# Weight block sums of seven-product tiles: from four GpSimd instructions to four transfers that add into SBUF

## The chip, the cores and the metric

The kernel runs on one core of one Trainium2 chip. The metric is the device time of one execution in microseconds; three runs of the kernel before give 1016.14, 1017.87 and 1018.72 us, median 1017.87. The engines are named as in the profile: PE (TensorE, the matrix products; PEld its weight loads), DVE (VectorE), ACT (ScalarE), POOL (GpSimd) and SP (SyncE). SP, ACT and POOL issue transfers (DMAs).

## The reference

One inference step of a one-layer decoder trunk, for 512 prompt tokens and 8 sample tokens together (520 columns), with width 1024. The mixer (gated recurrence and attention) is untouched by the change. What matters is the feed-forward part, with 2816 hidden features:

```
h2 = rms_norm(x, norm2_g) * (1.0 + sc2) + sh2
gu, up = jnp.split(h2 @ w_ffn_in, 2, axis=-1)
x = x + g2 * ((jax.nn.silu(gu) * up) @ w_ffn_out)
```

All inputs are float32.

## The kernel before

Activations lie with features on the 128 partitions and the 520 tokens along the row. Each float32 factor is split into a rounded part and a rest (`hi`, `lo`), and each product of two factors is three matmuls: hi·hi, lo·hi, hi·lo. A weight block is split by a cast on ACT (L270) and a subtraction on DVE (L271), in `split_four`, into a tile `wb` that holds four 128x128 blocks of `hi` and four of `lo`. The token factors are split the same way in `split`.

The feed-forward input product is done in 22 tiles of 128 hidden features (`jt` 0 to 21): each needs 128 gate columns and 128 up columns of `w_fi`, both 1024 rows deep. Tiles 0 to 3 are done plainly. Tiles 4 to 21, the fast tiles, use a scheme with seven products of half the depth in place of eight. A tile's weights form four blocks: A11 and A12 are the gate columns, rows 0-511 and 512-1023; A21 and A22 the up columns, rows 0-511 and 512-1023. The tokens likewise: `b1` and `b2` are features 0-511 and 512-1023 of `h2`, each with a left and a right half of 260 tokens (`L_`, `R_`). The scheme needs four sums of weight blocks (S1 to S4) and four sums of token blocks. The token sums are made once, for all tiles, by POOL in `h2_blocks` (four calls of four instructions, L1638 to L1644), then split by `split_blocks`. The weight sums are made in each tile by four POOL instructions (L261 to L264) into two buffers `ws`, when the tile's first block is split. Seven products (`BLOCKS`: A11, S2, S3, S1, A12, A22, S4), 12 matmuls each, accumulate into four PSUM banks X, Y, W, Z (`fi4x`, `fi4y` ... in the profile, the number being that of the tile). `fast_tile` combines the banks between the products, on DVE and ACT: after S1, Z is copied to `cp`, u2 is added to Z, and Y is written from `cp` and W; A22 then accumulates into W.

Between the seven products stand joined products: parts of the output product with `w_fo`, of 24 matmuls (`fo` in the profile, placed by the table `JOIN`): two in each of the tiles 4 to 16 and in 21, one in each of 17 to 20.

The order is set in the following way. The code asks for loads by `load_chunks` some 22 us, and for splits by `split_upto` some 11 us, ahead of use, by a reckoning of the matmuls in between (`reach`); a scheduler then puts each engine's instructions into one fixed order, and an engine goes through its own queue in that order, waiting where an operand or a buffer isn't there. Raw weights (`wraw`, 512 KB gate plus 512 KB up) alternate between two buffers, so a tile's load waits until the block A22 of the tile two before is split. The buffers `ws`, the raw joined weights of `w_fo`, the pairs `h2r` that `h2_blocks` reads, and earlier tiles share one ring of seven buffers (tag `pg`). All these loads go through SP's queue.

Of the kernel before, what the change touches and what calls it, by code (L numbers as in the profile page):

```python
# [8 lines left out]
F32 = mybir.dt.float32  # L9
# [3 lines left out]
ALU = mybir.AluOpType  # L13
# [11 lines left out]
KT = 8  # L25
# [40 lines left out]
def kernel(ctx, tc, xT, par, gates, b_f, cst, cse, own, cache_k, cache_v, cache_lf, pt,  # L66
# [3 lines left out]
    pe, act, dve, pool, sp = nc.tensor, nc.scalar, nc.vector, nc.gpsimd, nc.sync  # L70
# [3 lines left out]
    wp = ctx.enter_context(tc.tile_pool(name="wp", bufs=3))  # L74
    pgp = ctx.enter_context(tc.tile_pool(name="pgp", bufs=7))
# [79 lines left out]

    for c in range(len(chunks)):
        whole(c)
    joined = set()
    for jt in range(FF // 128):
        c = len(chunks)  # L160
        chunks.append(cols(w_fi, 128 * jt, 128) + cols(w_fi, FF + 128 * jt, 128))
        if jt < GROUP:
            whole(c)
            continue
        for name in BLOCKS:
            units.append((c, name, 4))
            if name in JOIN[jt]:
                g, i = JOIN[jt][name]
                if i % 2 == 0:
                    joined.add(len(chunks))  # L170
                    chunks.append(cols(w_fo, 128 * i, 256, 128 * GROUP * g, GROUP))
                units.append((max(joined), 128 * (i % 2), GROUP))
# [28 lines left out]
    def load_chunks(upto):  # L201
        while state["dma"] < len(chunks) and state["dma"] <= upto:
            c = state["dma"]
            if c in joined:
                raw = pgp.tile([128, GROUP, 256], F32, name="wraw", tag="pg")
            else:
                raw = wp.tile([128, KT, 256], F32, name="wraw", tag="wraw", bufs=2)
            o = 0
            for src, r0, nk, c0, n in chunks[c]:
                sp.dma_start(raw[:, :nk, o:o + n],  # L210
                             src[r0:r0 + nk * 128, c0:c0 + n].rearrange("(k p) c -> p k c", p=128))
                o += n
            raws[c] = raw
            state["dma"] += 1


    after = {}
# [4 lines left out]
    def split_upto(n):  # L222
        while state["split"] < len(units) and state["split"] <= n:
            m = state["split"]
            c, o, nk = units[m]
            load_chunks(c)
            raw = raws[c]
            state["split"] += 1
            if isinstance(o, str):
                splits[m] = split_block(raw, o)  # L230
                continue
            if c in joined:
                splits[m] = split_four(raw[:, :, o:o + 128])
                continue
            his, los = [], []
            step = 4 if m in in_heap else KT
            for k0 in range(0, nk, step):
                k1 = min(nk, k0 + step)
                if m in in_heap:
                    hi = slot("whs", 512, F32R).rearrange("p (k c) -> p k c", c=128)  # L240
                    lo = slot("wls", 512, F32R).rearrange("p (k c) -> p k c", c=128)
                else:
                    hi = wp.tile([128, KT, 128], F32R, name="whi", tag="whi", bufs=3)
                    lo = wp.tile([128, KT, 128], F32R, name="wlo", tag="wlo", bufs=3)
                src = raw[:, k0:k1, o:o + 128]
                state["act"] = act.copy(hi[:, :k1 - k0], src)  # L246
                with held(m):
                    state["last"] = dve.tensor_tensor(lo[:, :k1 - k0], src, hi[:, :k1 - k0].bitcast(F32), ALU.subtract)  # L248
                his += [hi[:, k] for k in range(k1 - k0)]
                los += [lo[:, k] for k in range(k1 - k0)]  # L250
            splits[m] = (his, los)

    blocks = {}

    def split_block(raw, name):
        if name == "A11":
            a11, a12, a21, a22 = (raw[:, k:k + 4, o:o + 128] for o in (0, 128) for k in (0, 4))
            s12, s34 = (pgp.tile([128, 8, 128], F32, name="ws", tag="pg") for _ in range(2))
            s1, s2, s3, s4 = s12[:, :4], s12[:, 4:], s34[:, :4], s34[:, 4:]
            blocks.update(A11=a11, A12=a12, A22=a22, S1=s1, S2=s2, S3=s3, S4=s4)  # L260
            pool.tensor_tensor(s1, a21, a22, ALU.add)  # L261
            pool.tensor_tensor(s2, s1, a11, ALU.subtract)
            pool.tensor_tensor(s3, a11, a21, ALU.subtract)
            pool.tensor_tensor(s4, a12, s2, ALU.subtract)  # L264
        return split_four(blocks[name])

    def split_four(src):
        state["tag"] = "wlo" if state.get("tag") == "whi" else "whi"
# [301 lines left out]
    raw = wraw()  # L570
# [1063 lines left out]
    def h2_blocks(k):  # L1634
        b1, b2 = h2raw[k], h2raw[k + 4]
        u, w = slot("u"), slot("w")
        with tc.issue_after(state["blocks"].ins) if k != 3 else nullcontext():
            first = pool.tensor_tensor(w[:, R_], b2[:, R_], b1[:, R_], ALU.subtract)  # L1638
        if k == 3:
            state["blocks"] = first  # L1640
        with tc.issue_after(state["blocks"].ins):
            pool.tensor_tensor(u[:, L_], b1[:, R_], b1[:, L_], ALU.subtract)
            pool.tensor_tensor(w[:, L_], b2[:, R_], u[:, L_], ALU.subtract)
            pool.tensor_tensor(u[:, R_], b2[:, L_], w[:, L_], ALU.subtract)  # L1644
        traw[k] = u, w

    def split_blocks(k0):
# [10 lines left out]
    def fast_tile(jt, ac):  # L1658
# [9 lines left out]
        for m_, name in enumerate(BLOCKS):  # L1668
            n = begin()
            hi, lo = splits[n]  # L1670
            for k in range(4):
                ah, al = h2_block(name, k)
                for m, (wt, at) in enumerate(((hi, ah), (lo, ah), (hi, al))):
                    state["mm"] = pe.matmul(into[name], lhsT=wt[k], rhs=at, start=m_ < 4 and k == 0 and m == 0,
                                            stop=k == 3 and m == 2, skip_group_check=m_ > 3)
            if name == "A11":
                act.copy(cp[:, L_], X)
            elif name == "S2":
                add(u2, cp[:, L_], Y)
            elif name == "S3":  # L1680
                add(W, u2, W)
            elif name == "S1":
                act.copy(cp[:, R_], Z)  # L1683
                add(Z, u2, Z)
                add(Y, cp[:, R_], W)
            elif name == "A12":
                act.activation(sw[:, L_], X, AF.Silu)
            elif name == "A22":
                close(W, L_)
            elif name == "S4":  # L1690
                act.activation(sw[:, R_], Z, AF.Silu)
                close(Y, R_)
            run_later(n)
            if name in JOIN[jt]:
                g, i = JOIN[jt][name]
                product(f"fo{g}_{i}", ac[GROUP * g:GROUP * g + GROUP], lambda j, b_, i=i: residual(i, b_, 5, j))
# [97 lines left out]
```

## Time and profile before

| what | us | 
|---|---|
| runs shown (three) | 1016.14, 1017.87, 1018.72 |
| the profiled execution: its span, first to last instruction | 1016.4 |
| PE busy | 994.3 (98%) |
| DVE busy | 797.3 (78%) |
| ACT busy | 547.5 (54%) |
| POOL busy | 327.6 (32%) |
| first fast tile's first product, on PE | from about 697 |
| last joined and output products, to the end | from about 970 |

The profiled execution's own device time isn't listed apart from the three; its span is what the page gives. The page has busy times by engine, busy shares in 40 slices of the span, the chain of work that ended last, the costliest groups of instructions, and the DMA issues. Other views of the same trace list instructions in order of time, waits, and busy times in a window. In a row of the timeline stand the start, the duration, the engine, the line of the kernel and out<-in by the program's names, and in brackets how long the engine was idle before and what ended that. The trace moved 206.97 MB at a mean of 204 GB/s, with the DMA engines less used in the feed-forward part than before it.

### The profile page before, as it was taken

Reading aid. Unit: us, or ns where it says so; the run is one execution under the profiler, and the core shown is the slowest. Engines: PE = TensorE matmul, PEld = TensorE weight load, DVE = VectorE, ACT = ScalarE, POOL = GpSimd, SP = SyncE. Lnnn points to the kernel's source line nnn. Section 1 sums busy time; section 2 is a strip of 40 time slices with the busy share of each in tenths; the row PEclk is TensorE's granted clock in tenths of the full one; section 3 lists DMA queues with packets and bytes.
Section 4 is the critical chain, followed back from the end, with each engine's and each line's share of the span. In section 5 each row is a group of like instructions: output and inputs, shape, how many; then the busy total and the mean of one; then the engine's idle time right before and its main releaser. Section 6 shows DMA issues by size and latency. Waiting matters only on the chain.

```text
span 1016.4 us, 21281 instructions
## 1 busy us (share of the span) xinstructions
PE 994.3 (98%) x8012; PEld 921.1 (91%) x8012; DVE 797.3 (78%) x1423; ACT 547.5 (54%) x1128; POOL 327.6 (32%) x415
## 2 busy tenths in 40 slices
PE   5999999999999999999999999999999999999996
PEld 2799999999998988888888888999999999999996
DVE  5559999998999888886655544869988888888764
ACT  4534576848761576777783233554444444445553
POOL 0346111121143245653400001583442442425112
PEclk9999999999999999999999999999999999999998
DMA  9798857788879998995867995324234243233122
GB/s 325 250 324 279 242 189 202 243 261 278 281 250 345 331 312 286 321 294 190 251 216 269 319 340 186 84 74 115 81 108 125 63 125 98 70 104 105 63 64 85
DMA packets 164378, 206.97 MB, mean 204 GB/s; under 512 B 9827, under 2 KB 125043, under 8 KB 164211
## 3 DMA queue, kind: packets, MB, share of 16 engines
q1 hardware_dynamic: 147634, 152.78, 48.1%
q0 software_dynamic: 12960, 46.41, 13.8%
q10 hardware_dynamic: 3680, 6.42, 1.7%
q8 instruction: 63, 1.03, 0.4%
q14 instruction: 41, 0.33, 0.1%
HBM read 192.49 MB, written 13.09 MB: 202 GB/s over the span
## 4 chain that ended last, share of the span: by engine, by line
PE 93%; DMA 2%; DVE 2%; ACT 1%; issue 0%; SPq 0%; POOL 0%; DVEq 0%; POOLq 0%; ACTq 0%
PE fo L307 12%; PE k L307 5%; PE wo L307 5%; PE gb L307 5%; PE gr L307 5%; PE v L307 5%; PE ga L307 5%; PE xr L307 5%; PE pb L307 4%; PE pv L839 3%; PE pa L307 3%; PE po L1302 2%; PE qp L542 2%; PE q L542 2%; PE ada L374 2%; PE ptt L1268 2%
## 5 line engine op out<-in xcount | busy, mean ns | idle before, releaser
L246 ACT CAST whi<-wraw 128x1024 fp32r<-128x1024 f32 (+1 forms) x79 | 82.0, 1039 | 113.6 <-PE pb L307 34.3
L248 DVE TENSOR_TENSOR wlo<-wraw,whi 128x1024 fp32r<-128x1024 f32 (+1 forms) x79 | 99.1, 1256 | 19.0 <-ACT whi L246 16.6
L307 PE MATMUL fo<-ach,wb 128*128 128x260 f32 x512 | 93.4, 283 | 0.0
L270 ACT CAST wb<-ws 128x512 fp32r<-128x512 f32 x72 | 44.7, 621 | 86.0 <-PE fo L307 58.9
L700 POOL DMA_DIRECT2D pg<-in_cache_k_dram x74 | 39.6, 536 | 143.1 <-DVE S L751 62.6
L271 DVE TENSOR_TENSOR wb<-wraw,wb 128x512 fp32r<-128x512 f32 x86 | 76.4, 889 | 4.7 <-ACT wb L270 3.9
L307 PEld LDWEIGHTS fo<-ach,wb 128*128 128x128 f32 x512 | 78.9, 188 | 0.0
L271 DVE TENSOR_TENSOR wb<-ws,wb 128x512 fp32r<-128x512 f32 x72 | 68.7, 954 | 12.6 <-ACT wb L270 11.0
L261 POOL TENSOR_TENSOR ws<-wraw 128x512 f32<-128x512 f32 x18 | 24.4, 1353 | 153.2 <-DMA wraw<-in_w_fi_dram 104.1
L307 PE MATMUL fo<-acl,wb 128*128 128x260 f32 x256 | 72.2, 282 | 0.0
L270 ACT CAST wb<-wraw 128x512 fp32r<-128x512 f32 x86 | 53.5, 622 | 31.4 <-ACT cp L1683 6.2
L750 DVE TENSOR_TENSOR pg<-pg,qb 128x1024 f32<-128x1024 f32 x48 | 57.9, 1221 | 2.5 <-DMA pg<-in_cache_k_dram 2.5
L751 DVE TENSOR_REDUCE S<-pg 128x16 f32<-128x1024 f32 x48 | 57.4, 1209 | 0.2
L1259 POOL TENSOR_SCALAR p<-p,mu 128x128 f32<-128x128 f32 (+3 forms) x28 | 38.4, 1381 | 53.0 <-DVE mu L1255 47.1
L307 PEld LDWEIGHTS fo<-acl,wb 128*128 128x128 f32 x256 | 48.2, 188 | 0.0
L1253 ACT ACTIVATE p<-p,mu 128x128 f32<-128x128 f32 (+3 forms) x64 | 35.4, 554 | 18.2 <-DVE mu L1252 18.0
L307 PE MATMUL v<-hh,whi 128*128 128x260 f32 x128 | 38.2, 298 | 0.8 <-ACT row L819 0.5
L307 PE MATMUL k<-hh,whi 128*128 128x260 f32 x128 | 37.3, 292 | 0.0
L307 PE MATMUL pb<-oh,whi 128*128 128x260 f32 x128 | 37.1, 290 | 0.2 <-ACT oh L1360 0.2
L307 PE MATMUL gb<-hh,whi 128*128 128x260 f32 x128 | 37.0, 289 | 0.0
L307 PE MATMUL v<-hl,whi 128*128 128x260 f32 x128 | 36.9, 288 | 0.0
L307 PE MATMUL v<-hh,wlo 128*128 128x260 f32 x128 | 36.9, 288 | 0.0
(1101 smaller groups left out, 3957.3 us busy)
## 6 DMA issues: line engine op xcount, KB each, us to landing
araw<-in_ada_w_dram SPq DMA_DIRECT2D x48, 512.0 KB, 7.6
wraw<-in_w_fi_dram SPq DMA_DIRECT2D x44, 512.0 KB, 5.3
pg<-in_cache_k_dram POOLq DMA_DIRECT2D x42, 512.0 KB, 6.2
pg<-in_cache_v_dram SPq DMA_DIRECT2D x42, 512.0 KB, 5.5
wraw<-in_w_in_dram SPq DMA_DIRECT2D x34, 512.0 KB, 6.4
wraw<-in_w_in_dram SPq DMA_DIRECT2D x11, 1024.0 KB, 8.5
pg<-in_cache_v_dram POOLq DMA_DIRECT2D x22, 512.0 KB, 6.1
pg<-in_cache_k_dram POOLq DMA_DIRECT2D x32, 256.0 KB, 5.9
```

Source lines behind the costliest of these rows:

```text
L246: state["act"] = act.copy(hi[:, :k1 - k0], src)
L248: state["last"] = dve.tensor_tensor(lo[:, :k1 - k0], src, hi[:, :k1 - k0].bitcast(F32), ALU.subtract)
L270: state["act"] = act.copy(t[:, :4], src)
L271: state["last"] = dve.tensor_tensor(t[:, 4:], src, t[:, :4].bitcast(F32), ALU.subtract)
L307: state["mm"] = pe.matmul(out[:, :t1 - t0], lhsT=wt[k], rhs=at, start=k == 0 and m == 0, stop=k == nk - 1 and m == 2)
L542: state["mm"] = pe.matmul(b[:, :HALF], lhsT=wt, rhs=at[:, t0:t1], start=k == 0 and m == 0, stop=k == 3 and m == 2)
L700: done.append(eng.dma_start(pg, cache[bass.ds(r, 1), :, c0:c1].rearrange("a p c -> (a p) c")))
L750: dve.tensor_tensor(pg, pg, q, ALU.mult)
L751: last = dve.tensor_reduce(S[r // 2][:, c:c + H], pg.rearrange("p (h d) -> p h d", d=DH), AX.X, ALU.add)
L839: pe.matmul(pv[0][32 * gq:32 * gq + 32, :], lhsT=pw[r][:, c:c + 32], rhs=pgs[gq // 2][:, 512 * hf:512 * hf + 512], start=j == 0, stop=j == ...
L1253: act.activation(p[:, :n + 128], p[:, :n + 128], AF.Exp, bias=mu[:, 0:1], scale=-1.0, accum_out=mu[:, 1:2])
L1259: (pool.tensor_scalar(p, p, mu[:, 2:3], None, ALU.mult) if a and i + 1 < KT else act.activation(p, p, AF.Copy, scale=mu[:, 2:3]))
```

## The change

The sums of weight blocks are no longer computed on POOL. A fast tile now makes four loads in place of two: the up block into the raw buffer, its rows 512-1023 (A22) a second time into a buffer `s1`, the gate block into the raw buffer, and the gate block a second time into a buffer that holds `s2` (rows 0-511, A11) and `s4` (rows 512-1023, A12). Then POOL issues four transfers of 256 KB inside SBUF that add to what lies at their target: A21 into `s1`, `s1` into `s2`, A11 into A21 (in the raw buffer itself, which becomes S3), and `s2` into `s4`. For the sums to be additions only, the scheme's signs are turned: S2 is S1 + A11 and no longer S1 - A11, S3 is A21 + A11 in place of A11 - A21, S4 is A12 + S2 in place of A12 - S2. The token sums and two of the combinations in `fast_tile` change sign to match. The buffers `s1` and `s2`/`s4` are taken when the load is asked for, no longer when the first block is split.

```
+            state["dma"] += 1
+            if c in fast:
+                raws[c] = load_fast(c)
+                continue
...
+    def load_fast(c):
+        raw = wp.tile([128, 2, KT, 128], F32, name="wraw", tag="wraw", bufs=2)
+        rows = [src[:, c0:c0 + n].rearrange("(k p) c -> p k c", p=128) for src, _, _, c0, n in chunks[c]]
+        s1, s24 = (pgp.tile([128, m, 4, 128], F32, name="ws", tag="pg") for m in (1, 2))
+        s1, s2, s4 = s1[:, 0], s24[:, 0], s24[:, 1]
+        a11, a12, a21, a22 = (raw[:, o, k:k + 4] for o in range(2) for k in (0, 4))
+        sp.dma_start(raw[:, 1], rows[1])
+        sp.dma_start(s1, rows[1][:, 4:])
+        sp.dma_start(raw[:, 0], rows[0])
+        sp.dma_start(s24.rearrange("p m k c -> p (m k) c"), rows[0])
+        pool.dma_start(s1, a21, accum_op=ALU.add)
+        pool.dma_start(s2, s1, accum_op=ALU.add)
+        pool.dma_start(a21, a11, accum_op=ALU.add)
+        pool.dma_start(s4, s2, accum_op=ALU.add)
+        return dict(A11=a11, A12=a12, A22=a22, S1=s1, S2=s2, S3=a21, S4=s4)
...
-                splits[m] = split_block(raw, o)
+                splits[m] = split_four(raw[o])
...
-            s12, s34 = (pgp.tile([128, 8, 128], F32, name="ws", tag="pg") for _ in range(2))
...
-            pool.tensor_tensor(s1, a21, a22, ALU.add)
-            pool.tensor_tensor(s2, s1, a11, ALU.subtract)
-            pool.tensor_tensor(s3, a11, a21, ALU.subtract)
-            pool.tensor_tensor(s4, a12, s2, ALU.subtract)
...
-            first = pool.tensor_tensor(w[:, R_], b2[:, R_], b1[:, R_], ALU.subtract)
+            first = pool.tensor_tensor(w[:, R_], b1[:, R_], b2[:, R_], ALU.subtract)
...
-            pool.tensor_tensor(u[:, L_], b1[:, R_], b1[:, L_], ALU.subtract)
-            pool.tensor_tensor(w[:, L_], b2[:, R_], u[:, L_], ALU.subtract)
-            pool.tensor_tensor(u[:, R_], b2[:, L_], w[:, L_], ALU.subtract)
+            pool.tensor_tensor(u[:, L_], b1[:, L_], b1[:, R_], ALU.subtract)
+            pool.tensor_tensor(w[:, L_], w[:, R_], b1[:, L_], ALU.subtract)
+            pool.tensor_tensor(u[:, R_], b2[:, L_], w[:, L_], ALU.add)
...
-                add(W, u2, W)
+                dve.tensor_tensor(W, W, u2, ALU.subtract)
...
-                add(Y, cp[:, R_], W)
+                dve.tensor_tensor(Y, W, cp[:, R_], ALU.subtract)
```

The change moves instructions in two queues. The orders of PE, DVE and ACT stay as they were, but that S3 is split out of `wraw`.

POOL's queue before, at the start of the fast tiles. `h2r` are the pairs of token blocks, `u` and `w` their sums (L1638 to L1644), `wraw_9988` the raw block of tile 4:

```order
L1506 TENSOR_TENSOR h2r_9412<-h2r_9412,mod_102 128x2x8
L1638 TENSOR_TENSOR w_9962<-h2r_9412,h2r_9386 128x260
L1642 TENSOR_TENSOR u_9961<-h2r_9386 128x260
...
L1643 TENSOR_TENSOR w_9980<-h2r_9412,u_9979 128x260
L261 TENSOR_TENSOR ws_10143<-wraw_9988 128x512
L1644 TENSOR_TENSOR u_9979<-h2r_9412,w_9980 128x260
L262 TENSOR_TENSOR ws_10143<-ws_10143,wraw_9988 128x512
L263 TENSOR_TENSOR ws_10144<-wraw_9988 128x512
L264 TENSOR_TENSOR ws_10144<-wraw_9988,ws_10143 128x512
```

The same place now (`ws_9989` is S1 of tile 4, `ws_9990` its S2 and S4; a row `DMA` is the issue of a transfer that adds; the lines are those of the changed kernel):

```order
L1512 TENSOR_TENSOR h2r_9412<-h2r_9412,mod_102 128x2x8
L230 DMA ws_9989<-wraw_9988 128x512
L1644 TENSOR_TENSOR w_9962<-h2r_9386,h2r_9412 128x260
L1648 TENSOR_TENSOR u_9961<-h2r_9386 128x260
...
L1649 TENSOR_TENSOR w_9980<-w_9980,h2r_9386 128x260
L231 DMA ws_9990<-ws_9989 128x512
L1650 TENSOR_TENSOR u_9979<-h2r_9412,w_9980 128x260
L232 DMA wraw_9988<-wraw_9988 128x512
L233 DMA ws_9990<-ws_9990 128x512
L230 DMA ws_10149<-wraw_10148 128x512
```

The first sum of tile 4 has moved from behind 15 of the 16 token block instructions to ahead of all of them; the second stands where the first stood.

SP's queue before, from tile 4 to tile 7 (`wraw_9988`, `10140`, `10392`, `10599`, two loads each), with the joined loads from `w_fo` between them:

```order
L210 DMA wraw_9988<-in_w_fi_dram 128x8x128 x2
L210 DMA wraw_10316<-in_w_fo_dram 128x4x256
L210 DMA wraw_10140<-in_w_fi_dram 128x8x128 x2
L210 DMA wraw_10448<-in_w_fo_dram 128x4x256
L210 DMA wraw_10392<-in_w_fi_dram 128x8x128 x2
L210 DMA wraw_10655<-in_w_fo_dram 128x4x256
L210 DMA wraw_10599<-in_w_fi_dram 128x8x128 x2
```

Now, from tile 5 (`wraw_10148`) to tile 7 (`wraw_10605`); L227 is the load of S1's buffer, L229 that of S2 and S4's, L226 and L228 the raw block:

```order
L227 DMA ws_10397<-in_w_fi_dram 128x4x128
L226 DMA wraw_10148<-in_w_fi_dram 128x8x128
L228 DMA wraw_10148<-in_w_fi_dram 128x8x128
L229 DMA ws_10398<-in_w_fi_dram 128x8x128
L215 DMA wraw_10460<-in_w_fo_dram 128x4x256
L226 DMA wraw_10396<-in_w_fi_dram 128x8x128
L228 DMA wraw_10396<-in_w_fi_dram 128x8x128
L227 DMA ws_10606<-in_w_fi_dram 128x4x128
L229 DMA ws_10607<-in_w_fi_dram 128x8x128
L215 DMA wraw_10669<-in_w_fo_dram 128x4x256
L226 DMA wraw_10605<-in_w_fi_dram 128x8x128
L228 DMA wraw_10605<-in_w_fi_dram 128x8x128
```

A tile's second copies (`ws`) and its joined load now stand ahead of its raw block; the joined load of tile 7 (`wraw_10669`) is the seventh buffer of the ring after `ws_10150`, which holds S2 and S4 of tile 5, and takes that buffer over.

More of the change, by code (lines that the diff above doesn't have):

```diff
@@ L157 @@
         whole(c)
-    joined = set()
+    joined, fast = set(), set()
     for jt in range(FF // 128):
@@ L164 @@
             continue
+        fast.add(c)
         for name in BLOCKS:
@@ L213, in load_chunks @@
             raws[c] = raw
-            state["dma"] += 1
+    def load_fast(c):
[13 more added lines that the diff above has]
+        return dict(A11=a11, A12=a12, A22=a22, S1=s1, S2=s2, S3=a21, S4=s4)
     after = {}
@@ L251, in split_upto @@
             splits[m] = (his, los)
[L253 to L257, printed above, removed]
-            s12, s34 = (pgp.tile([128, 8, 128], F32, name="ws", tag="pg") for _ in range(2))
[L259 to L265, printed above, removed]
     def split_four(src):
```

## The prediction

> **What bounds the kernel now.** I read the page first: its busy times, its slices and its chain. Then I asked what TensorE (PE) waits for from 640 us to the end, which is the stretch that the change touches, and for the busy times in a few tiles of it. In the windows rows the numbers behind the range are its length, then busy us and instructions of PE, PEld, DVE, ACT and POOL, then the granted clock, the DMA share and GB/s.
>
> ```profile
> PE 994.3 (98%) x8012; PEld 921.1 (91%) x8012; DVE 797.3 (78%) x1423; ACT 547.5 (54%) x1128; POOL 327.6 (32%) x415
> PE   5999999999999999999999999999999999999996
> DMA  9798857788879998995867995324234243233122
> PE 93%; DMA 2%; DVE 2%; ACT 1%; issue 0%; SPq 0%; POOL 0%; DVEq 0%; POOLq 0%; ACTq 0%
> ...
> PE r L1593 <- ACT sq L1581: 0.2, 1, 0.2
> ...
> 715.80:731.60 15.80, 15.80 (x134) 15.80 (x133) 14.10 (x27) 7.27 (x15) 6.41 (x5) 1.00 0.36 101
> 905.00:918.00 13.00, 13.00 (x110) 13.00 (x109) 11.09 (x23) 6.72 (x15) 4.17 (x3) 1.00 0.31 82
> ```
>
> PE is busy 98% of the span and carries 93% of the chain. From 640 us on, its only recorded wait is 0.2 us, in the last norm. One fast tile with two joined products fills 15.8 us with 134 matmuls (0.118 us each) at granted clock 1.00; one with a single joined product takes 13 us. The change leaves the order, count and shapes of the matmuls as they are. So inside the fast tiles there is nothing to win: the question is whether the new block sums arrive in time, and that depends on how long an adding transfer takes.
>
> **What goes.** The four sums of a tile leave POOL's arithmetic:
>
> ```profile
> L261 POOL TENSOR_TENSOR ws<-wraw 128x512 f32<-128x512 f32 x18 | 24.4, 1353 | 153.2 <-DMA wraw<-in_w_fi_dram 104.1 <-DVE wb L271 19.5 <-DVE fi11y L1662 10.0
> L262 POOL TENSOR_TENSOR ws<-ws,wraw 128x512 f32<-128x512 f32 x18 | 27.3, 1516 | 0.0
> L263 POOL TENSOR_TENSOR ws<-wraw 128x512 f32<-128x512 f32 x18 | 29.8, 1656 | 0.0
> L264 POOL TENSOR_TENSOR ws<-wraw,ws 128x512 f32<-128x512 f32 x18 | 29.7, 1651 | 1.3
> L271 DVE TENSOR_TENSOR wb<-ws,wb 128x512 fp32r<-128x512 f32 x72 | 68.7, 954 | 12.6 <-ACT wb L270 11.0
> ```
>
> That is 24.4 + 27.3 + 29.8 + 29.7 = 111 us of POOL, 6.2 us a tile, none of it on the chain. DVE gains too: its split of one block took 0.69 us beside an idle POOL and up to 1.8 us beside a busy one (rows below), so some 20 us of DVE time go. PE waits for neither, so I cost both at nothing. The turned signs in the token blocks change no count and no shape: nothing.
>
> **What comes.** Two more loads a tile, 0.75 MB, and four adding transfers of 256 KB each. Each adding transfer is issued by POOL after its operands have landed, so a tile's S2 is ready two transfers after its raw block, S4 three. I call the time from POOL's turn to the landing L. No row of before adds in a transfer; the nearest are POOL's cache loads:
>
> ```profile
> 175.00:245.00 70.00, 70.00 (x579) 66.01 (x578) 62.92 (x78) 50.04 (x88) 12.67 (x24) 1.00 0.80 259
> L700 POOL DMA_DIRECT2D pg<-in_cache_k_dram x15 | 7.9, 528 | 40.9 <-DVE S L751 21.5 <-PE pv L839 16.4 <-DVE pg L750 1.7
> DMA to landing us min/median/max: 3.0/5.9/8.9
> q0 software_dynamic: 12960, 46.41, 13.8%
> ```
>
> POOL needs 0.53 us to issue one, and it landed after 3.0 us at best, 5.9 in the median and 8.9 at worst, with the DMA engines 80% busy. An addition reads two operands, but moves half of the bytes, inside SBUF, beside engines now 36% busy. The new traffic raises that: 0.36 of 15.8 us for 1.5 MB is 3.8 us per MB, so 2.25 MB take 8.5 us; 1 MB of additions at POOL's price (13.8% of 1016.4 us for 46.41 MB, 3.0 us per MB) takes 3 us, or 6 if counted twice. A tile then holds the DMA engines 11.5 to 14.5 of 15.8 us. So I keep 3.0 and 8.9 as ends and take **L = 5.0**, nearer to the median, since much of a chain runs between the loads.
>
> The Trainium skill, "DMA: Bandwidth & Descriptors", section "Anatomy of one DMA — SWDGE (gpsimd) path", gives about 2.0 us plus the bytes at 436 GB/s for a transfer from POOL, so an estimated 2.6 us for 256 KB; by that price L would be 3.1 with the issue, every term below nothing, and the time 1017.9. No row here shows it for additions.
>
> **The first fast tile (tile 4).** POOL's first addition stands in its queue ahead of all the token block work of `h2_blocks`, and the second behind 15 of those 16 instructions.
>
> ```profile
> 665.39 0.93 POOL L1638 TENSOR_TENSOR w<-h2r 128x260 f32<-128x260 f32 x1 [2.09 <-issue]
> 680.10 1.31 POOL L261 TENSOR_TENSOR ws<-wraw 128x512 f32<-128x512 f32 x1
> 671.23 0.99 SPq L210 DMA_DIRECT2D wraw<-in_w_fi_dram  x2
> DMA to landing us min/median/max: 3.3/5.3/6.3
> 686.60 0.61 ACT L270 CAST wb<-ws 128x512 fp32r<-128x512 f32 x1
> 690.01 1.78 DVE L271 TENSOR_TENSOR wb<-ws,wb 128x512 fp32r<-128x512 f32 x1
> 691.31 5.72 PE fiu L307 x48
> 709.99 1.45 PE fi4w L1674 x12
> ```
>
> Before, POOL began the blocks at 665.4 and had 15 of them done at 680.1: 14.7 us. Now it stands until tile 4's raw block has landed: issued at 671.2, plus about 4 (the row says 3.3 to 6.3), plus the issue, 675.8. S2's addition is issued at 690.5 by the old durations, at some 688.7 if they shrink beside a DVE with less to do. Behind POOL wait the splits of the token blocks on ACT and DVE (the S2 block's cast is ahead of A11's on ACT, as 686.60 and 690.01 show), and behind these PE's first fast matmul at 691.31 + 5.72 = 697.0. S2 lands at 690.5 + 5.0 = 695.5; a cast of 0.6 and four short DVE instructions, 2.5 us, end A11's split at 698.6: **PE stalls 1.6 us**, or 0 with the shorter blocks. I take 1.0. Each us of L adds a us.
>
> **The second (tile 5).** Its buffers come from the token pairs that `h2_blocks` reads, free at 692 instead of 682.6, and SP issues its raw block behind them. With 1.75 MB ahead of or in the raw block, at 3.8 us per MB, it lands at about 699; S2 is there at 699 + 2L = 709.
>
> ```profile
> 705.73 0.62 ACT L270 CAST wb<-ws 128x512 fp32r<-128x512 f32 x1 [0.87 <-PE fi4z L1674]
> 707.33 0.43 DVE L1662 TENSOR_TENSOR fi4y<-fi4w,cp 128x260 f32<-128x260 f32 x1
> ```
>
> ACT casts S2 of tile 5 at 705.7. Queued behind that cast are the copy of fi4z and, on DVE, the sum that reads fi4w, done at 707.8; PE's A22 product overwrites fi4w at 710.0. So a delay of up to 2.2 us costs nothing. The cast is 3.3 us late, less the 1.0 that PE has lost already: 0.1. With the landing half a us off, I take 0.5.
>
> **The other tiles.** Here the loop is: raw buffer free, load, two additions, cast of S2, A22 of the tile before.
>
> ```profile
> 719.22 1.00 SPq L210 DMA_DIRECT2D wraw<-in_w_fi_dram  x2
> 720.01 0.69 DVE L271 TENSOR_TENSOR wb<-ws,wb 128x512 fp32r<-128x512 f32 x1
> 725.15 1.30 POOL L261 TENSOR_TENSOR ws<-wraw 128x512 f32<-128x512 f32 x1 [8.82 <-DMA wraw<-in_w_fi_dram]
> 737.43 0.62 ACT L270 CAST wb<-ws 128x512 fp32r<-128x512 f32 x1 [0.86 <-PE fi6z L1674]
> 739.02 0.43 DVE L1662 TENSOR_TENSOR fi6y<-fi6w,cp 128x260 f32<-128x260 f32 x1
> 741.65 1.45 PE fi6w L1674 x12
> 932.82 0.99 SPq L210 DMA_DIRECT2D wraw<-in_w_fi_dram  x2
> 947.57 0.62 ACT L270 CAST wb<-ws 128x512 fp32r<-128x512 f32 x1 [0.86 <-PE fi20z L1674]
> 949.17 0.43 DVE L1662 TENSOR_TENSOR fi20y<-fi20w,cp 128x260 f32<-128x260 f32 x1
> 948.90 2.89 PE fo L307 x24
> ```
>
> Tile 7's load was issued at 719.2 and POOL saw it 5.9 us later. Now SP has the joined load of w_fo ahead of it, whose buffer is free when DVE has split S4 of tile 5, at 720.7. Raw and w_fo are again 1 MB up to the first addition: 726.6. Then 2L up to the cast at 737.4: it is in time for L up to 5.4, and with the 2.2 us between fi6y's end (739.45) and A22 (741.65), PE sees nothing up to **L = 6.5**. In the tiles of 13 us (16 to 21) the raw block does not wait for S4, and lands about 5.4 after 932.8: 2L must fit from 938.2 to 947.6, and 2.2 more: **L = 5.8**. At 5.0 both terms are nothing. The end of the program keeps its length.
>
> **Sum.** Span 1016.4 + 1.0 + 0.5 = 1017.9. The median of the three runs shown, 1017.87, is 1.5 above this profiled span, so the time is 1019.4.
>
> **The rivals.** (1) *Slow additions.* Past L = 5.6 the terms pass 3 us: at 5.9 tile 4 costs about 2, tile 5 about 1.5, the short tiles 0.2 every second tile: 1022. At 7 it is 3, 2.6, then 2 x (7 - 6.5) at every second of ten long tiles (5 us) and 2 x (7 - 5.8) at every second of six short ones (7 us): 18, or 1036. For it: 5.9 is the median of the nearest rows, and an addition reads twice. Against: those rows are of a stretch with 80% DMA. (2) *The DMA engines become the bound.* If additions cost 12 us per MB, four times POOL's loads, a tile needs 8.5 + 12 = 20.5 us of DMA against 15.8: 4.7 us times 18 tiles, 1102; by latency alone 8.9 gives 2 x 2.4 five times and 2 x 3.1 three times, with 9 at the start 52, or 1070. Nothing in the rows asks for such a price; nothing excludes it. (3) *POOL's issues are held up by DVE.* If an issue waits out DVE's instruction (up to 1.8 us, row at 690.01), L is 6.8 and the time, worked out as in rival 1, 1032. Against it: between 175 and 245 us DVE was busy 62.9 of 70 us and the 15 issues still took 0.53 us each. The Trainium skill, "SBUF — State Buffer", section "SBUF: two separate sides", warns of this: while DVE works in a mode that takes the port it shares with GpSimd, transfers issued from GpSimd get no descriptors. The trace disagrees for the DVE work of that stretch. (4) *Faster*, because DVE and POOL are relieved: the wait row leaves 0.2 us to win, 1017.7; a gain beyond 0.3% would need PE to run quicker than 0.118 us a matmul.
>
> **How the numbers follow.** The forecast, L up to 5.6: 0.52. Rival 1: 0.27. Rival 2, with L past 7.2: 0.14. Rival 3: 0.04. Faster: 0.03. A measurement of this kernel tells some 0.3%, 3 us, from no change: same 0.52, slower 0.27 + 0.14 + 0.04 = 0.45, faster 0.03. The range for 8 in 10 runs from 1015.5 (nothing lost, a run at the lower end) to 1038 (L a little past 7); beyond lie most of rival 2 and a little of the others. The likeliest case's own range is 1016 to 1021.
>
> **What would show it.** Right: POOL's additions land within 5.6 us, PE has a gap of 0 to 3 us near 697 and none after 730, POOL idles before its first block until 675, and DVE's busy time falls. Wrong: PE waits for DVE sums or ACT casts once every second tile (rival 1), a DMA row near 1.00 in the tiles (rival 2), POOL issues well over 0.53 us (rival 3). The tile 4 step is wrong if POOL's blocks begin near 665 as before.

## The result, and the profile after

The changed kernel takes 1025.55 us (median of 5 runs, 1023.73 to 1027.52), the kernel before 1017.87 (5 runs, 1016.14 to 1021.92): a ratio of 1.0070, 95% interval 1.0049 to 1.0091. That is 7.7 us more, where the forecast was 1.5. A second measurement later (experiment 10) gave 1.0053 (1.0035 to 1.0071). The profiled execution took 1025.87 us with a span of 1024.2, against 1016.4 before.

The page of the changed kernel: busy times, the DMA engines in the 40 slices of the span, and the queue that holds POOL's transfers (packets, MB, share of the 16 engines' span).

```profile
PE 998.2 (97%) x8012; PEld 923.3 (90%) x8012; DVE 757.7 (74%) x1423; ACT 546.1 (53%) x1128; POOL 275.4 (27%) x415
DMA  9798867888879998996767994349899999999522
q0 software_dynamic: 23328, 65.29, 25.7%
```

DVE is busy 40 us less than before and POOL 52 us less, and nothing of it reaches the time. The DMA row, 2 to 4 in the fast tiles before, stands at 8 or 9 there. From 640 us on, PE now waits four times where it waited once (total us, times, longest):

```profile
PE fi4w L1680 <- DVE fi4y L1691: 3.5, 1, 3.5
PE fi20w L1680 <- DVE fi20y L1691: 0.8, 1, 0.8
PE fi18w L1680 <- DVE fi18y L1691: 0.7, 1, 0.7
PE r L1599 <- ACT sq L1587: 0.2, 1, 0.2
```

The first is the place of the prediction's step on tile 5: the A22 product of tile 4, held by the DVE sum that reads `fi4w`. In the timeline (start, duration, engine, line, what; in brackets the idle time ahead and what ended it) the chain reads from POOL's first addition on:

```profile
675.87 0.95 POOL L230 DMA_DIRECT2D ws<-wraw  x1 [12.19 <-ACT ach L1525]
676.52 1.09 POOL L1644 TENSOR_TENSOR w<-h2r 128x260 f32<-128x260 f32 x1
687.06 1.20 POOL L231 DMA_DIRECT2D ws<-ws  x1
690.16 0.67 SPq L226 DMA_DIRECT2D wraw<-in_w_fi_dram  x1
693.57 0.62 ACT L276 CAST wb<-ws 128x512 fp32r<-128x512 f32 x1 [1.51 <-issue]
700.08 0.87 POOL L230 DMA_DIRECT2D ws<-wraw  x1 [5.43 <-issue]
703.76 0.87 POOL L231 DMA_DIRECT2D ws<-ws  x1 [2.81 <-DMA ws<-wraw]
704.24 1.59 SPq L228 DMA_DIRECT2D wraw<-in_w_fi_dram  x1
711.73 0.62 ACT L276 CAST wb<-ws 128x512 fp32r<-128x512 f32 x1 [6.48 <-DMA ws<-ws]
713.33 0.43 DVE L1691 TENSOR_TENSOR fi4y<-fi4w,cp 128x260 f32<-128x260 f32 x1
713.90 0.48 PE L1680 MATMUL fi4w<-tuh,wb 128*128 128x260 f32 x2 [3.52 <-DVE fi4y L1691]
```

POOL stands 12.2 us until tile 4's raw block is there (the row names a cast on ACT that ends at about the same time; the half that POOL adds was issued at 671.2 and landed at 675.2). Then it does the token blocks, and tile 5's raw block is issued at 690.16. The half of it that S1 reads landed at 698.3; what held POOL's issue until 700.08, 1.8 us later, no view names (in most later tiles 0.5 to 0.6 us lie between the two). S1 is added from 700.08 to 703.7, S2 from 703.76 to 711.6: 3.7 and then 7.8 us, the second beside the loads that SP issues for the next tiles. ACT has stood 6.5 us for it; the DVE sum and PE follow.

What comes right behind the wait is in the windows (length; busy us and instructions of PE, PEld, DVE, ACT, POOL; granted clock, DMA share, GB/s):

```profile
714.00:718.00 4.00, 4.00 (x21) 4.00 (x22) 3.13 (x9) 0.89 (x2) 0.86 (x1) 0.57 0.77 141
718.00:722.00 4.00, 4.00 (x36) 4.00 (x35) 2.53 (x6) 2.56 (x6) 1.75 (x2) 1.00 0.77 188
730.00:880.00 150.00, 150.00 (x1253) 150.00 (x1252) 107.82 (x239) 69.14 (x144) 33.78 (x39) 1.00 0.95 215
885.00:955.00 70.00, 69.21 (x574) 68.79 (x574) 48.35 (x106) 33.37 (x71) 16.54 (x19) 1.00 0.95 214
```

For 4 us the clock is 0.57, and PE does 21 matmuls in the first row where it does 36 in the second: 0.43 x 4.00 = 1.7 us lost on top of the 3.5. In the long tiles PE is busy 150 of 150 us beside DMA engines at 0.95; in the short ones it is not, at the same share.

The span grew by 7.8 us. By the starts of the first product of tiles 4, 5, 16 and 21 (696.9, 712.7, 886.8, 954.5 before; 697.3, 718.4, 892.5, 962.6 after) 0.4 of it lies ahead of tile 4, **5.3 in tile 4**, nothing in tiles 5 to 15, **2.4 in tiles 16 to 20**, and the end is 0.3 shorter.

### The profile page after: what moved, and what is told of

Its sections match the earlier page's. It is cut to its first block, busy times and chain, and to the rows that moved or that the text cites. A ratio compares the mean times of both kernels' runs of the same rounds, so it can differ in the third digit from the quotient of the medians.

```text
span 1024.2 us, 21489 instructions
## 1 busy us (share of the span) xinstructions
PE 998.2 (97%) x8012; PEld 923.3 (90%) x8012; DVE 757.7 (74%) x1423; ACT 546.1 (53%) x1128; POOL 275.4 (27%) x415
## 5 line engine op out<-in xcount | busy, mean ns | idle before, releaser
L276 ACT CAST wb<-wraw 128x512 fp32r<-128x512 f32 x104 | 64.5, 621 | 70.6 <-PE fo L313 21.2
L277 DVE TENSOR_TENSOR wb<-wraw,wb 128x512 fp32r<-128x512 f32 x104 | 71.8, 692 | 26.0 <-ACT wb L276 23.9
L276 ACT CAST wb<-ws 128x512 fp32r<-128x512 f32 x54 | 33.5, 620 | 72.9 <-PE fo L313 38.6
L277 DVE TENSOR_TENSOR wb<-ws,wb 128x512 fp32r<-128x512 f32 x54 | 37.4, 692 | 28.3 <-ACT wb L276 27.2
L1265 POOL TENSOR_SCALAR p<-p,mu 128x128 f32<-128x128 f32 (+3 forms) x28 | 38.3, 1378 | 51.4 <-DVE mu L1261 46.4
L230 POOL DMA_DIRECT2D ws<-wraw x18 | 15.7, 874 | 87.4 <-DVE wb L277 36.2
L231 POOL DMA_DIRECT2D ws<-ws x18 | 15.8, 880 | 80.2 <-issue 31.9
```

Of the source, the lines that this page charges most:

```text
L230: pool.dma_start(s1, a21, accum_op=ALU.add)
L231: pool.dma_start(s2, s1, accum_op=ALU.add)
L276: state["act"] = act.copy(t[:, :4], src)
L277: state["last"] = dve.tensor_tensor(t[:, 4:], src, t[:, :4].bitcast(F32), ALU.subtract)
L1265: (pool.tensor_scalar(p, p, mu[:, 2:3], None, ALU.mult) if a and i + 1 < KT else act.activation(p, p, AF.Copy, scale=mu[:, 2:3]))
```

## The experiments

Each was measured in five rounds against the kernel before on its own chip. The table gives the ratio with its interval, and from the profiled execution the time from the start of one tile's first product to that of the other.

| kernel | ratio | 4 to 5 | 5 to 6 | 6 to 16 | 16 to 21 |
|---|---|---|---|---|---|
| before | 1 | 15.8 | 15.8 | 158.3 | 67.7 |
| changed | 1.0070 (1.0049-1.0091) | 21.1 | 15.8 | 158.3 | 70.1 |
| 1 all sums on POOL | 1.0058 (1.0043-1.0073) | 21.5 | 15.9 | 158.3 | 67.6 |
| 2 tiles 4, 5 on POOL | 1.0087 (1.0074-1.0101) | 22.4 | 15.8 | 158.3 | 71.8 |
| 3 loads, POOL adds | 1.0061 (1.0044-1.0078) | 21.7 | 15.8 | 158.3 | 67.7 |
| 4 gap filled | 1.0058 (1.0037-1.0078) | 18.7 | 15.9 | 158.2 | 69.3 |
| 5 tile 4's additions behind | 1.0067 (1.0043-1.0092) | 15.8 | 18.3 | 158.3 | 69.3 |
| 6 all on POOL, tile 4 behind | 1.0015 (1.0006-1.0024) | 17.3 | 15.8 | 158.3 | 67.7 |
| 7 as 5, short tiles on POOL | 1.0041 (1.0029-1.0053) | 15.8 | 17.4 | 158.3 | 67.7 |
| 8 as 5, short tiles half | 1.0022 (1.0011-1.0033) | 15.8 | 18.0 | 158.3 | 67.6 |
| 9 as 5, S1 on POOL, no load | 1.0003 (0.9993-1.0013) | 17.0 | 15.9 | 158.3 | 67.6 |
| 10 changed kernel again | 1.0053 (1.0035-1.0071) | 20.4 | 15.8 | 158.3 | 70.1 |
| 11 as 5, raw block first | 1.0168 (1.0150-1.0186) | 15.8 | 17.0 | 164.2 | 78.7 |
| 12 as 5, S1 on POOL, loads kept | 0.9996 (0.9987-1.0006) | 15.9 | 15.8 | 158.3 | 67.7 |

The first theory was: one late S2 at the start, because its addition lands beside loads (3.5 us of waiting and 1.7 of halved clock), and full DMA engines in the short tiles (2.4).

**1. All sums on POOL**, at the changed kernel's place in its queue:

```
-        sp.dma_start(s1, rows[1][:, 4:])
-        sp.dma_start(s24.rearrange("p m k c -> p (m k) c"), rows[0])
-        pool.dma_start(s1, a21, accum_op=ALU.add)
...
+        pool.tensor_tensor(s1, a21, a22, ALU.add)
+        pool.tensor_tensor(s2, s1, a11, ALU.add)
+        pool.tensor_tensor(a21, a21, a11, ALU.add)
+        pool.tensor_tensor(s4, a12, s2, ALU.add)
```

> All four sums of every fast tile go back to POOL's arithmetic, with the turned signs, the changed kernel's buffers and its place in POOL's queue; no extra loads. Theory (the loss comes from the additions by transfer): the time of the kernel before, 1018 (1016.5 to 1020), ratio 1.000, no wait of PE above 0.5 us after 640 us. Rival (the turned signs, the separate S3 or the sums' new place in the queues cost something): it stays above 1022.

A miss for the theory; the time is the rival's. The end is cured, as expected, but tile 4 costs 5.7 us without a single adding transfer. Its one new wait of PE, and then POOL's first rows in the timeline:

```profile
PE fi4x L1687 <- DVE wb L284: 3.9, 1, 3.9
```

```profile
674.38 1.71 POOL L229 TENSOR_TENSOR ws<-wraw 128x512 f32<-128x512 f32 x1 [11.87 <-ACT ach L1532]
676.05 0.75 POOL L1651 TENSOR_TENSOR w<-h2r 128x260 f32<-128x260 f32 x1
```

POOL stands here too for 11.9 us with the token blocks queued behind the first sum, as the prediction said of its tile 4 step. A wait of 3.9 us and a halved clock follow. The changed kernel shares this place in the queue, so the place became a suspect.

**2. Tiles 4 and 5 on POOL.** The edit of experiment 1 for these two tiles alone.

> Only the sums of tiles 4 and 5 go back to POOL's arithmetic (with their extra loads gone); tiles 6 to 21 add by transfer. Theory (one late sum at the start of the stage costs 3.5 us of waiting and then 1.7 us of a halved clock, the short tiles the other 2.5): 5.2 us less than the changed kernel, 1020.3 (1019 to 1021.5), no wait at fi4w, clock 1.00 between 712 and 720 us, the waits at fi18w and fi20w still there. Rival (any first tile whose additions run beside loads is late): the same stall one or two tiles later, at fi5w or fi6w, and 1024 to 1026.

Neither theory: the wait at `fi4w` goes, and that of experiment 1 at `fi4x` comes (3.9 us, with the clock halved for 6.8 us, part of it within the wait). The stall of the short tiles is larger, with a cut of the clock behind it (the wait, and the window that follows it):

```profile
PE fi18w L1687 <- DVE fi18y L1698: 2.3, 1, 2.3
```

```profile
932.00:936.00 4.00, 3.93 (x20) 3.93 (x21) 2.45 (x8) 2.03 (x4) 0.12 (x1) 0.57 0.79 146
```

**3. All loads, POOL adds.**

```
-        pool.dma_start(s1, a21, accum_op=ALU.add)
+        pool.tensor_tensor(s1, s1, a21, ALU.add)
...
```

> The two extra loads of each tile stay, and POOL's arithmetic adds onto the loaded copies in place of the transfers. Theory (the chain of two additions is late, not the loads): two sums on POOL take 2.7 us after the raw block where two transfers took 11.6, so the wait at fi4w goes: 1018 to 1020, DMA share in the long tiles about 0.55. Rival (the extra loads delay the raw blocks by themselves): waits at fi4w and in the short tiles remain, 1022 to 1025.

The extra loads by themselves cost the long and the short tiles nothing (158.3, 67.7). The start again loses 5.9 us, in waits of 0.4, 0.8 and 2.9 us with a halved clock after the last: three of tile 4's sums now stand ahead of the token blocks, which begin at 678.4. The time is in the rival's range, but not for the rival's reason: no wait at `fi4w` and none in the short tiles is left. Both expectations left POOL's place out.

**4. The gap filled.**

```
+            if name == "A12" and jt == GROUP:
+                for k in range(8):
+                    for wt, at in ((hi, ah), (lo, ah), (hi, al)):
+                        state["mm"] = pe.matmul(X, lhsT=wt[k % 4], rhs=at, start=False, stop=False,
+                                                skip_group_check=True)
```

> The changed kernel with 24 more matmuls in tile 4, just ahead of the product that waits 3.5 us: the last token block of A12 is added into its sum eight more times over, so that tile's output differs from the reference's. 24 matmuls take 2.9 us. Theory (the wait for the sum is fixed in time and the halved clock follows from TensorE standing idle): the wait shrinks to 0.6 us, the clock stays at 1.00, and the time falls by 1.7 to 1023.9. Rival 1 (the clock is cut there for another reason): 1025.5, with the cut in the clock row. Rival 2 (the late sum moves along with PE's work): 2.9 us more, 1028.4.

1.0058, where the expected 1023.9 was 1.0059 of 1017.87. The profiled execution has no wait left at `fi4w` and the clock at 1.00 there; tile 4 is longer by just the 2.9 us of the added matmuls. That fits a cut of the clock that comes from the gap, but does not show it: in this execution the cast of S2 came 12.9 us after the start of tile 4, 14.4 in the changed kernel, so the gap would have been some 1.8 us without the added work. The seven runs fall into two groups, four of 1020.35 to 1021.62 with a mean granted clock of 0.997 and three of 1024.15 to 1025.57 with 0.993 to 0.996; the profile is of the first. So the 1.7 us is read from the windows, not from this ratio.

**5. Tile 4's additions behind the token blocks.** In `load_fast` the four additions of tile 4 are kept back, and issued at A11's split:

```
+                with tc.issue_after(state["tokens"].ins):
+                    todo.pop(c)()
```

(`tokens` is the last instruction of `h2_blocks`.)

> The changed kernel, with the four adding transfers of tile 4 alone issued by POOL behind the sixteen token block instructions in place of ahead of them; tiles 5 to 21 as in the changed kernel. New theory (the loss at the start comes from POOL's queue: the first addition stands there until tile 4's raw block has landed, and holds up the token blocks by 10 us, and behind them tile 5's buffers and loads): POOL begins the blocks near 665 us, no wait at fi4w, no halved clock after it, and 5 us less than the changed kernel; what the short tiles lose (2.4) stays: 1.0024 of before. Rival (an addition that lands in 8 us beside loads is the cause, wherever POOL stands): S2 of tile 5 is late by 2 us or more as before, 1.005 to 1.007.

POOL does its blocks early, tile 5's raw block is issued at 682.4 instead of 690.2, tile 4 takes 15.8 us, and the wait at `fi4w` is gone; but the time can't be told from that of the changed kernel (1.0067 here, 1.0070 and 1.0053 there). The wait is now one tile later, at `fi5w`, and a short tile still waits. PE's waits, and the loop of tile 6 in the timeline:

```profile
PE fi5w L1692 <- DVE fi5y L1703: 2.2, 1, 2.2
PE fi19w L1692 <- DVE fi19y L1703: 1.2, 1, 1.2
```

```profile
702.51 0.48 SPq L229 DMA_DIRECT2D wraw<-in_w_fi_dram  x1
713.26 0.86 POOL L234 DMA_DIRECT2D ws<-wraw  x1 [9.57 <-issue]
718.32 0.86 POOL L235 DMA_DIRECT2D ws<-ws  x1 [4.20 <-DVE rs L1493]
725.16 0.62 ACT L288 CAST wb<-ws 128x512 fp32r<-128x512 f32 x1 [5.11 <-PE fo L325]
```

The raw block is issued when the one before last has been read (two buffers). It takes 10.7 us to POOL's turn (8.9 to the landing of the half that S1 reads, then 1.9 that no view explains), S1's addition 5.1, S2's 6.7: 22.5 us from issue to landing, at 725.0. The cast follows 0.2 us later, though its row names PE. The cast of S2 was due 8.8 us after the start of tile 5, as in the tiles beside it, at 720.8, and PE could bear 2.2 us more: 20.5 us after the issue. So the second theory, **C**: this loop is too long at the start of the stage, wherever POOL's blocks stand. The six runs go from 1018.74 to 1027.37; the two slowest have a mean granted clock of 0.992 and 0.993, the profiled one (1021.16) 0.995, which suggests cuts behind longer waits in them, but no trace shows those.

**6. All on POOL, tile 4 behind.** Experiment 1 with the edit of experiment 5.

> All four sums of all tiles on POOL's arithmetic, without the extra loads, as in the first experiment, but those of tile 4 behind the token blocks. New theory: its 3.9 us wait at fi4x and the halved clock go, ratio to before 1.000 (0.9985 to 1.0015). Rival (turned signs or the separate S3 cost 5 us at the start): 1.005 as in the first experiment.

The wait at `fi4x` and the cut are gone: 1.0015 instead of 1.0058. POOL's place costs 4.4 us when POOL makes the sums. The other 1.5 us (2.4 at most) lie in tile 4, with recorded waits of 0.6 and 0.2, and stay open. The turned signs and the separate S3 don't cost them by themselves: experiment 12 has both, and its tile 4 takes 15.9 us.

**7. As 5, short tiles on POOL.** Experiment 1's edit where `jt >= LAST` (16).

> As the first of these four, and the sums of the short tiles (16 to 21) on POOL's arithmetic without their extra loads; so tiles 4 to 15 alone add by transfer. New theory (start by POOL's queue, tail by transfers in 13 us tiles, nothing in the long tiles): 1.000 (0.9985 to 1.0015), with the DMA share still above 0.9 from 730 to 880 us. Rival (the filled DMA engines cost the long tiles something as well): 1.002 or more with waits between 730 and 880.

**8. As 5, short tiles half.** Where `jt >= LAST`:

```
+            sp.dma_start(s2, rows[0][:, :4])
+            pool.dma_start(s1, a21, accum_op=ALU.add)
+            pool.dma_start(s2, s1, accum_op=ALU.add)
+            pool.tensor_tensor(a21, a21, a11, ALU.add)
+            pool.tensor_tensor(s4, a12, s2, ALU.add)
```

> As the first of these four, but in the short tiles only S1 and S2 add by transfer, in the same chain; S3 and S4 are POOL's arithmetic, and S4's extra load is gone. That takes 0.25 MB of loads and two additions of 0.25 MB from each 13 us tile. Theory D (the short tiles lose because their transfers fill the DMA engines): no waits at fi18w to fi20w, 1.000 to 1.001. Rival L (two additions one after the other don't fit into 13 us, whatever the share): the waits stay at 0.7 to 2.3 us, 1.002 or more.

Both missed their expected time, since the wait at `fi5w` stays (1.3 and 1.9 us), but both have a clean end. The windows of the short tiles, experiment 7's and then experiment 8's:

```profile
885.00:955.00 70.00, 70.00 (x586) 70.00 (x585) 56.72 (x110) 36.02 (x75) 22.74 (x16) 1.00 0.31 88
```

```profile
885.00:955.00 70.00, 70.00 (x585) 70.00 (x585) 58.60 (x109) 35.46 (x75) 21.98 (x19) 1.00 0.60 149
```

Experiment 8 keeps the chain of two additions, and with the share at 0.60 no wait is left. So what the short tiles lose comes with the filled DMA engines, not with two additions in a row by themselves. S3 and S4 left the transfers too, so this run doesn't tell a late S2 from a late S3. Experiment 7's profiled execution is the quickest of its six runs (1017.31; the others 1018.40 to 1022.03), and experiment 8's ran from 1017.18 to 1022.13: how long the wait at `fi5w` was in the slower ones no trace shows.

**9. S1 on POOL, its load gone, tile 4 behind.**

```
-        sp.dma_start(s1, rows[1][:, 4:])
...
-            pool.dma_start(s1, a21, accum_op=ALU.add)
+            pool.tensor_tensor(s1, a21, a22, ALU.add)
```

> Tile 4's additions behind the token blocks, as in the fifth experiment, and in all tiles S1 is POOL's sum of the raw block (1.3 us) in place of an adding transfer onto its own load (4.2 to 5.1 us); S2, S3 and S4 still add by transfer, and S1's load of 0.25 MB is gone. Theory C (from the issue of a raw block, whose buffer is free only when the tile before last has been read, to the landing of S2 there are some 21 us; in the fifth experiment tile 6 took 22.6, 10.7 of it the raw block and 11.9 the two additions): without 3.5 us of it no wait at fi5w and none above 0.5 us in the short tiles, 1.000 to 1.002. Rival R (what is late is the landing of the raw blocks behind the other loads): waits of 1 us or more stay, 1.004 or more.

As C expects: 1.0003, and no wait above 0.3 us after 640. But the DMA share of the long tiles fell to 0.75, and tile 6's raw block (raw_6) was at POOL after 4.0 us, so rival R wasn't excluded; experiments 11 and 12 are for that. Tile 4 takes 17.0 us, with recorded waits of 0.3 and 0.2; the rest of that stays open, as in experiment 6.

**10. The changed kernel again.**

> The changed kernel as it is, once more on the chip of these runs, for comparison with the fifth experiment (1.0067, 1.0043 to 1.0092). Theory C: 1.006 to 1.008 with the wait at fi4w again, 2.5 us or more. If moving the additions of tile 4 gained its 5 us after all, this one stands at 1.010 or more here.

1.0053, with 2.8 us at `fi4w`: a little below C's 1.006 to 1.008, and far from 1.010. Moving tile 4's additions gains nothing by itself that these intervals can tell.

**11. Raw block first.**

```
-        sp.dma_start(s1, rows[1][:, 4:])
...
+        last = sp.dma_start(raw[:, 0], rows[0])
+        with tc.issue_after(last.ins):
+            sp.dma_start(s1, rows[1][:, 4:])
+            sp.dma_start(s24.rearrange("p m k c -> p (m k) c"), rows[0])
```

> As the fifth experiment, but the copies for S1 and for S2 and S4 of each tile are loaded behind that tile's raw block, where they went a tile ahead of it before; the same bytes and additions. Rival R (the raw block lands late because copies and the joined load go ahead of it): raw_6 lands in 7 to 8 us, the waits shrink, 1.002 to 1.004. Theory C (the loop is full, and what goes ahead of the chain's first addition counts): the copies now stand in the chain themselves, so nothing is gained or the waits come back in every second tile, 1.007 to 1.02.

1.0168, as C expects, and the only kernel that loses time in the long tiles: 5.9 us there, and 11.0 in the short ones, where PE waits 6.1 us at once and the clock is halved for 6.8. At the start rival R has a point: tile 6's raw block is there 7.5 us after its issue, and the wait at `fi5w` falls from 2.2 to 0.9. But the copies, loaded a tile ahead before, now stand in the loop, and it is too long in about every second tile. PE's longest waits:

```profile
PE fi18w L1693 <- DVE fi18y L1704: 6.1, 1, 6.1
PE fi16w L1693 <- ACT wb L289: 1.5, 1, 1.5
PE fi12w L1693 <- DVE fi12y L1704: 1.4, 1, 1.4
PE fi14w L1693 <- DVE fi14y L1704: 1.3, 1, 1.3
PE fi7w L1693 <- DVE fi7y L1704: 1.2, 1, 1.2
PE fi10w L1693 <- DVE fi10y L1704: 1.2, 1, 1.2
```

**12. S1 on POOL, all loads kept.**

```
-            pool.dma_start(s1, a21, accum_op=ALU.add)
+            pool.tensor_tensor(s1, s1, a21, ALU.add)
```

> As the fifth experiment (tile 4's additions behind the token blocks, all loads in their order), with one change: POOL's arithmetic adds onto the loaded copy for S1 (1.3 us) where a transfer did (4.2 to 5.1 us). All loads stay, so the raw blocks land as late as there, some 10 us after their issue at the start. Theory C (the sum of landing and additions is too long by a little): 3.5 us less is enough, no wait above 0.5 us at fi5w, 1.000 to 1.003. Rival R (the raw blocks land too late behind the copies, and only the missing load helped before): waits of 1 us or more stay, 1.004 or more.

0.9996 (0.9987 to 1.0006): the whole loss is gone by one adding transfer less per tile, with every load in its place and tile 4's additions behind the token blocks. Nothing is gained on the kernel before. Tile 6's loop, and the windows of the long and the short tiles:

```profile
698.88 0.37 SPq L229 DMA_DIRECT2D wraw<-in_w_fi_dram  x1
705.20 1.28 POOL L234 TENSOR_TENSOR ws<-ws,wraw 128x512 f32<-128x512 f32 x1 [11.56 <-DMA wraw<-in_w_fi_dram]
706.78 0.87 POOL L235 DMA_DIRECT2D ws<-ws  x1 [0.30 <-POOL ws L234]
```

```profile
730.00:880.00 150.00, 150.00 (x1253) 150.00 (x1253) 112.52 (x237) 68.43 (x141) 38.52 (x39) 1.00 0.86 203
885.00:955.00 70.00, 70.00 (x586) 70.00 (x585) 52.69 (x108) 35.55 (x76) 16.08 (x16) 1.00 0.75 175
```

S2's addition landed after 4.1 us, so the loop took 12.0 us where experiment 5's took 22.5. Only 3.5 of these 10.5 us are the replaced transfer itself: the half of the raw block that S1 reads landed 2.7 us sooner (6.2 after its issue, not 8.9), POOL began 0.1 us after that and not 1.9, and S2's addition landed 2.6 us sooner. The expectation that the raw block would be as late as before was wrong. With a transfer less the others land sooner, and the raw buffer is free earlier (raw_6 was issued 11.4 us ahead of tile 5's first product, 9.5 in experiment 5). How much is the chain and how much the fuller DMA engines, these runs don't separate.

## Why the prediction came out as it did

The time fell near the middle of the range of 1015.5 to 1038, but 6.2 us above the forecast of 1019.4 and outside the 1016 to 1021 of the likeliest case, no change, which was wrong. That the range held owes something to luck: its upper end stood for additions of a little over 7 us each, late in every second tile; the medians measured are 5.0 and 3.9, and the 7.7 us are made up otherwise.

- **What bounds the kernel, and what goes.** Right. PE is still busy 97%, and the relief of DVE and POOL is worth nothing.
- **Tile 4, 1.0 us.** It cost 0 in the changed kernel. That POOL stands until the raw block has landed was right to the tenth (675.8 foreseen, 675.87 measured), but the blocks took 0.70 us each, 10.5 us in all for fifteen, where 12.9 to 14.7 was taken, and S2 was landed at 693.5 instead of 695.5.
- **Tile 5, 0.5 us.** This step failed by its size, not its mechanism. The cast of S2 came at 711.73 instead of 705.73: 6.0 us late, less the slack of 2.2 and the 0.4 by which the tile began later, 3.4; measured 3.5. The sum had put the cast at 709: the raw block was there at 698.3, near the 699 taken, but POOL's turn came at 700.08, and the two additions took 3.7 + 7.8 = 11.5, not 2 x 5.0. The remark that "much of a chain runs between the loads" failed here, where SP has just issued the loads of two tiles. And the 1.0 us credited from tile 4 wasn't there.
- **The clock** was in no term, and no reason was given for leaving it out: 1.7 us behind the gap.
- **Long tiles, nothing up to L = 6.5.** Right: 158.3 us before and after. L was near enough in the mean. The views of the two chained additions of the changed kernel, S1's group first and then S2's, each with its landing times over the 18 tiles:

```profile
L230 POOL DMA_DIRECT2D ws<-wraw x18: 860/860/991, 675.9 to 947.4; - x18
...
DMA to landing us min/median/max: 3.4/5.0/7.7
```

```profile
L231 POOL DMA_DIRECT2D ws<-ws x18: 860/860/1200, 687.1 to 952.7; - x18
...
DMA to landing us min/median/max: 3.6/3.9/7.8
```

- **Short tiles, nothing up to L = 5.8.** Wrong, 2.4 us. The step asked only whether two additions fit, and compared the DMA engines' 11.5 to 14.5 us with tiles of 15.8 us alone. It also took tiles 16 to 21 for short, where only 17 to 20 last 13.0 us before. The queues of the changed kernel between 730 and 880 us (SP's loads, then POOL's additions: packets, MB, share of 16 engines):

```profile
q1 hardware_dynamic: 39812, 22.35, 52.1%
q0 software_dynamic: 5356, 9.75, 42.8%
```

  That is 3.5 us per MB of load, and 0.428 x 150 / 9.75 = 6.6 us per MB of addition, above the 3 to 6 allowed. A long tile then needs 2.36 MB x 3.5 + 1.05 MB x 6.6 = 15.2 of 15.8 us. A short one, with a joined load every second tile, needs 2.10 x 3.5 + 6.9 = 14.2 of 13.0 us: more than there is. So the mechanism of rival 2 fits the short tiles; its price of 12 us per MB was too high, and the long tiles stay just below it. Ahead of the wait at `fi18w` the two additions of tile 19 took 12.3 us (917.68 to 929.99), 6.2 each, above the 5.8 allowed. Ahead of that at `fi20w` those of tile 21 took only 9.9, but its raw block was issued 7.4 us ahead of tile 20, 8.7 before the change. What was delayed in between was also S3, which the step didn't look at, and POOL's queue behind S4:

```profile
930.52 0.86 POOL L233 DMA_DIRECT2D ws<-ws  x1 [4.74 <-DMA ws<-ws]
931.31 0.99 POOL L230 DMA_DIRECT2D ws<-wraw  x1
935.27 0.62 ACT L276 CAST wb<-wraw 128x512 fp32r<-128x512 f32 x1 [4.23 <-DMA wraw<-wraw]
```

- **Rival 1** had the right chain of engines. Its wait in every second tile came in the short ones (`fi18w`, `fi20w`); in the long ones it came once, at the start, where the raw block is late as well. **Rival 3**: the issues of the two chained additions do take more than 0.53 us, but nearly the same in all tiles (median 0.860, rows above), and 0.86 is also the least. Nothing shows that they wait for DVE, and 0.3 us more an issue explains none of the waits. Open is what POOL waited for in the 1.8 us ahead of tile 5's first issue.

## What to carry to other kernels

When a sum is moved from an engine to a transfer, add up the whole loop from the freeing of its buffer to its landing, in each stage apart and at the start of the stage most of all: a chain of two transfers fits on the average and fails where the loads of two tiles run together. Price the DMA engines against the shortest tile, not the usual one. Where such a loop is just too long, replacing one link may be enough, since the others get shorter with it: here one POOL sum of 1.3 us in place of one of four transfers gave back everything, with the first tile's sums moved behind the token blocks; without that move it was not tried.

## What the runs showed of the hardware

An addition inside SBUF held the DMA engines 6.6 us per MB at a share of 0.95 (5.8 in the short tiles of experiment 8, at 0.60), nearly twice the 3.5 of a load, which is the same without additions beside it (experiment 3: 51.4% of 150 us for 21.77 MB). The S1 additions of 256 KB landed 3.4 to 7.7 us after POOL's turn, 0.86 of it the issue. The Trainium skill, "DMA: Bandwidth & Descriptors", section "Anatomy of one DMA — SWDGE (gpsimd) path", gives by its fit an estimated 2.6 us, 3.5 with that issue: the quickest landing agrees, the median of 5.0 lies 1.5 above it.

From tile 4 to tile 21 the granted clock fell to a half with waits of PE of 6.1, 3.9 (twice), 3.5, 2.9, 2.8 and 2.3 us, and not with waits of 2.2 us or less. It stayed there for 3.4 us, or twice that with the 6.1 and one of the 3.9. In the changed kernel that adds half of the wait to its price. A long wait is not the only way to a cut: in the traces of eight of the fourteen kernels, before and after among them, the clock is also halved for 3.4 us at 461 us, in the mixer, where no wait of PE is above 0.3 us. That stands ahead of tile 4 and outside the table's stretches, but it lengthens a profiled span by up to 1.7 us. The Trainium skill, "TensorE: Matmul & The Clock Gate", section "Part 1: The HAM clock gate (the "warmup" mystery)", states that the clock is halved after an idle window of about 3.4 us, in windows that run freely; the cut is as long as one or two such windows here, but a wait of 2.3 us was enough for it.
